# FFN down projection: eight pairs of feature tiles by seven products instead of six, a new order of blocks, the last row of factors in halves

## The chip, the core and the metric

The kernel runs on one core of a Trainium2 chip. Its engines work side by side and are tied together by semaphores: TensorE (PE, with its weight loads shown apart as PEld), VectorE (DVE), ScalarE (ACT), GpSimd (POOL) and SyncE (SP), whose queue issues most transfers. SBUF is the working memory, PSUM holds matmul results (eight banks of 128x512 float32). The metric is the device time of one execution in microseconds (us); lower is better.

## The reference

One transformer layer on 256 latent tokens of width 2048, with 256 context tokens. Everything is float32. The part that matters here is the second half of the layer, the convolutional FFN:

```python
def conv_ffn(h, w_up, conv_w, conv_b, w_down):
    u = depthwise_conv(h @ w_up, conv_w, conv_b)      # width 2 * D_FF, D_FF = 5632
    a, g = jnp.split(u, 2, axis=-1)
    return (jax.nn.silu(g) * a) @ w_down              # (256, 5632) @ (5632, 2048)
...
    h = modulate(rms_norm(x, g_ffn_pre[l]), sh2, sc2)
    x = x + gt2 * rms_norm(conv_ffn(h, w_up[l], conv_w[l], conv_b[l], w_down[l]), g_ffn_post[l])
```

## The kernel before

The layer is one long program; TensorE is fed from its first microseconds to the last. In the order of time: modulation vectors, keys, values, queries, attention, branch products and gates, the output projection, then **FFN up** (from about 775 us to 1264 us) and **FFN down** (from 1264 us to the end).

*Precision.* A float32 matrix is used as a sum of two rounded parts, high and low. `split` (L133) makes them: ACT writes the high part (L137), DVE the low part, source minus high (L141). Each product then takes three matmuls: high by high, low activations by high weights, high activations by low weights (`product`, L1254, matmul at L1256).

*Weights.* They come in blocks of 1 MB (128x2048). `raw_block` (L123) loads one into one of four `raw` buffers; `halves` (L144) splits it into `wh` and `wl`, two buffers each, in two pieces of 128x1024. `block` (L192) hands out the block that is used now and has the next one split and the next three loaded.

*FFN up.* Of the 44 feature tiles of 128 each, `gate` (L1163) makes the gated activations. Tile j lands in `ff` (high and low part, 128 features by 256 tokens), from where it is the stationary operand of the down matmuls. Twelve tiles, J0 = 28 to 39, six pairs, go to `fs` instead, where `gate` stores, for each pair, seven 128x128 combinations of its four quarters (2 tiles by 2 halves of the tokens), four of them made in a small tile `st` by additions (L1183).

*FFN down.* The output, 256x2048, is made in two passes h = 0 and 1, each over two chunks c of 512 columns and two halves t of the tokens: four accumulators C[t, c] in PSUM. A pass takes 22 blocks, whose kinds stand in `SEQ` (L57):

- a **D** block (`direct`, L1260) holds four feature tiles for one chunk: 4 tiles x 2 halves t x 3 = 24 matmuls of 128x512;
- an **S** block (`fold`, L1267) holds one pair of tiles for both chunks. Done directly that would be 2 tiles x 2 chunks x 2 halves = 8 products; by a scheme of Strassen's kind it takes seven, 21 matmuls. Three use `wh`, `wl` as they are (the first 9 matmuls); four use sums of the block's quarters, `th`, `tl`. `folded` (L168) makes those: splits of 128x512 and 128x1024 for `wh`, `wl`, then four additions of 128x512 in place on the raw block (L177), then two splits of 128x1024 into `th`, `tl`, of which there is one buffer each. The seven products go to C[0,0], C[0,1], C[1,0] and four helpers X[1], X[5], X[6], X[7].

```python
SEQ = "DSDDSDDSDDSDDSDDSDDDDD"            # 57
def is_folded(j): return J0 <= j < J0 + 2 * NS   # 64
```

After the last S of a pass (the 17th block, n = 16) `sums_1` and `sums_2` (L1295, L1300) add the helpers up, with ACT and DVE, into the output rows `yg`. `close` (L1283) ends one accumulator: it adds the helper sum, squares with a running sum (ACT, L1291) for the norm, and multiplies by the row `grow` of factors (L1293). In pass 1 C[1,1] gets its helper sum by an addition in PSUM (L1316), before more matmuls go into it. Pass 1 ends with a tail (L1328): the last `lead` = 2 D blocks do t = 0 first, then t = 1, so that half of the output can be finished (`finish`, L1232: norm, residual `x1`, store) under the rest.

PE, DVE and ACT each run their instructions in the order that a scheduler fixed when the program was built; it may move an instruction of one block past those of the next.

Of the kernel before, what the change touches and what calls it, by code (L numbers as in the profile page):

```python
# [10 lines left out]
F32 = mybir.dt.float32  # L11
F32R = mybir.dt.float32r
AF = mybir.ActivationFunctionType
ALU = mybir.AluOpType

P = 128
D = 2048
KT = D // P
S = 256
# [6 lines left out]
FT = DFF // P  # L26
# [26 lines left out]
ND = 4  # L53
SW = (KT - ND) * P // 4
KW = (NKVA + NHB) * P
J0, NS = 28, 6
SEQ = "DSDDSDDSDDSDDSDDSDDDDD"  # L57


def direct_tile(j):  # L60
# [8 lines left out]
def layer_kernel(ctx, tc, xc, xt, ccol, crow, wm_sc, wm_sd, wm_sh, wm_b, cols, wk, wkt, ws, rope, mask_a, bias_b, out):  # L69
    nc = tc.nc  # L70
    sync = nc.sync

    cp = ctx.enter_context(tc.tile_pool(name="cp", bufs=1))
# [9 lines left out]


    col = cp.tile([P, NCOL], F32, name="col")
    cc = cp.tile([P, KT, 32], F32, name="cc")
    ident = cp.tile([P, P], F32, name="ident")
    modx = cp.tile([P, 64], F32, name="modx")
    gcol = cp.tile([P, 2, KT], F32, name="gcol")
# [27 lines left out]
    ggd = tc.dram_tile([2, KT, P], F32, name="ggd")  # L117
# [141 lines left out]
    def gain_row(i, dst):  # L259
        sync.dma_start(out=dst, in_=ggd[i].rearrange("a b -> (a b)").partition_broadcast(P))  # L260
# [10 lines left out]
    with ExitStack() as mx:  # L271
# [10 lines left out]
        with ExitStack() as at:  # L282
# [16 lines left out]
            st = kv.enter_context(ExitStack())  # L299
# [317 lines left out]
            for k in range(3, KT):  # L617
# [2 lines left out]
                        nc.vector.tensor_tensor(out=kT[:, NK1 + i], in0=pk[i][:], in1=rs[:], op=ALU.mult)  # L620
                whole(k)
            st.close()

# [525 lines left out]
        return u, add_halves(u[:], pu, f"u{f}")  # L1151

    def conv(u, f, i):
        a = cv.tile([P, S], F32, tag=f"a{i}", bufs=3 - i, name=f"a{f}")
        cw = [col[:, C_CW + 3 * f + q : C_CW + 3 * f + q + 1] for q in range(3)]
        nc.scalar.activation(a[:], u[:], AF.Identity, scale=cw[1], bias=col[:, C_CB + f : C_CB + f + 1])
        nc.vector.scalar_tensor_tensor(
            out=a[:, 1:], in0=u[:, : S - 1], scalar=cw[0], in1=a[:, 1:], op0=ALU.mult, op1=ALU.add)
        nc.vector.scalar_tensor_tensor(
            out=a[:, : S - 1], in0=u[:, 1:], scalar=cw[2], in1=a[:, : S - 1], op0=ALU.mult, op1=ALU.add)  # L1160
        return a

    def gate(j, a, g):  # L1163
        nc.scalar.activation(g[:], g[:], AF.Silu)
        nc.vector.tensor_tensor(out=a[:], in0=a[:], in1=g[:], op=ALU.mult)
        if not is_folded(j):
            d = direct_tile(j)
            split(ff[:, d, 0], ff[:, d, 1], a[:])
            return
        p, odd = divmod(j - J0, 2)  # L1170
        w = (1 + odd) * P
        hi, lo = (fs[:, p, q].rearrange("p i t -> p (i t)") for q in range(2))
        split(hi[:, odd * P : odd * P + w], lo[:, odd * P : odd * P + w], a[:, :w])
        if not odd:
            first[:] = [a]
            return
        a0, a1 = first[0][:, :P], first[0][:, P:]
        t = cv.tile([P, 4 * P], F32, tag="st", bufs=1, name=f"st{p}")
        t_ = [t[:, i * P : i * P + P] for i in range(4)]
        for o, x, y, op in (  # L1180
            (t_[2], a0, a1, ALU.subtract), (t_[0], a1, a[:, P:], ALU.add), (t_[1], t_[0], a0, ALU.subtract),
            (t_[3], a[:, :P], t_[1], ALU.subtract)):
            nc.vector.tensor_tensor(out=o, in0=x, in1=y, op=op)  # L1183
        split(hi[:, 3 * P :], lo[:, 3 * P :], t[:])
# [55 lines left out]

    first_wts = block(3)
    yg = yp.tile([P, 2, D], F32, name="yg2")
    grow = yp.tile([P, D], F32, name="grow2")
    gain_row(1, grow)
    down = [j for j in range(FT) if not is_folded(j)]
    for h in range(2):
        c0, c1 = 2 * h, 2 * h + 1
# [12 lines left out]
        def direct(wts, g, c, t):  # L1260
            for kk in range(4):
                j = direct_tile(down[4 * g + kk])
                product(
                    C[t, c], lambda i: ff[:, j, i, t * P : t * P + P], *wts, slice(kk * 512, kk * 512 + 512), (t, c),
                    stop=g == 7 and kk == 3)

        def fold(wts, p):  # L1267
            (wh, wl), (th, tl) = wts
# [11 lines left out]
        def add(out_, a, b):  # L1280
            nc.vector.tensor_tensor(out=out_, in0=a, in1=b, op=ALU.add)

        def close(t, c, part, after=None):  # L1283

            y = yg[:, t, cs[c]]
            if part:
                add(y, C[t, c][:], y)
            with ExitStack() as es:
                if after:
                    es.enter_context(tc.issue_after(after))  # L1290
                nc.scalar.activation(  # L1291
                    C[t, c][:] if part else y, y if part else C[t, c][:], AF.Square, accum_out=ss[:, t, c0 + c : c0 + c + 1])
            nc.vector.tensor_tensor(out=y, in0=y if part else C[t, c][:], in1=grow[:, cs[c]], op=ALU.mult)  # L1293

        def sums_1():  # L1295
            nc.scalar.activation(yg[:, 0, cs[0]], X[1][:], AF.Copy)
# [4 lines left out]
            add(yg[:, 0, cs[1]], X[5][:], yg[:, 1, cs[1]])  # L1301
            add(yg[:, 1, cs[1]], X[5][:], yg[:, 1, cs[0]])

        late, d, f, lead = [], 0, 0, 2 * h
        for n, kind in enumerate(SEQ[: len(SEQ) - lead]):
            wts = first_wts if h == n == 0 else block(3)
            if late:
                late.pop(0)()
            if kind == "S":
                fold(wts, f)  # L1310
                f += 1
                if f == NS:
                    late = [sums_1, sums_2, lambda: close(0, 0, True), lambda: close(1, 0, True)]
                    if h:
                        sync.dma_start(out=x1, in_=x1d)
                        late[2:] = [lambda: (close(0, 0, True), add(C[1, 1][:], C[1, 1][:], yg[:, 1, cs[1]]), close(1, 0, True))]  # L1316
            else:
                for t in range(2):
                    direct(wts, d % 8, d // 8, t)
                d += 1  # L1320
            if h and n == 4:
                warm_table(AF.Sqrt, "d", ss[:, 0, 0:1])
        if h == 0:
            for t in range(2):
                close(t, 1, True)
        else:
            wts, after = [], None
            for g in range(8 - lead, 8):  # L1328
                wts.append(block(3))
                direct(wts[-1], g, 1, 0)  # L1330
            for t in range(2):
                if t:
                    for i, g in enumerate(range(8 - lead, 8)):
                        direct(wts[i], g, 1, 1)
                close(t, 1, t == 0, after)
                after = finish(t)


# [30 lines left out]
def _layout(x, c, ctx, c_ctx, w_mod, b_mod, g_attn_pre, g_attn_post, g_ffn_pre, g_ffn_post,  # L1369
# [37 lines left out]
    def slabs(w, n):  # L1407
        k = 2048 // n
        return w.reshape(-1, k, P, w.shape[1] // n, n).transpose(3, 0, 2, 1, 4).reshape(-1, P, 2048)
# [22 lines left out]
    ws[B_UP + 5 : B_DN : 2] = u[FT + 2 :]  # L1432
    wd = f(w_down)[0].reshape(FT, P, D)
    down = [j for j in range(FT) if not is_folded(j)]
    d = slabs(wd[down].reshape(-1, D), 512).reshape(2, 16, P, 2048)
    for h in range(2):
        n, g = iter(range(16)), iter(range(NS))
        for i, kind in enumerate(SEQ):
            if kind == "D":
                ws[B_DN + h * len(SEQ) + i] = d[h, next(n)]  # L1440
            else:
                j = J0 + 2 * next(g)
                a, b = (wd[k][:, h * 1024 : h * 1024 + 1024].reshape(P, 2, 512) for k in (j, j + 1))
                ws[B_DN + h * len(SEQ) + i] = np.concatenate([a[:, 1], a[:, 0], b[:, 1], b[:, 0]], axis=1)
# [26 lines left out]
```

## Time and profile before

| | us |
|---|---|
| three runs: median (lowest to highest) | 1506.01 (1505.78 to 1507.14) |
| the profiled execution: its own time | 1505.69 |
| its span in the trace | 1503.9 |
| FFN down on PE: first to last matmul's start | 1264.2 to 1495.7 |

In the table of the span in 40 slices (each row one engine, a digit the busy share in tenths) PE and its clock stand at 9 throughout; DVE has 9s only within the first eleven slices:

```profile
PE   9999999999999999999999999999999999999997
DVE  4496897999988888877678887887888878777776
PEclk9999999999999999999999999999999999999999
```

A busy PE does not mean that it can go no faster, since matmuls overlap each other; how far apart their starts lie is what counts. Rows of a timeline read: start, length, engine, line, operation, what is written from what, how many in a row, and in brackets how long the engine was idle before and who ended it.

### The profile page before, as it was taken

The numbers are of one execution on the slowest core, as the hardware profiler recorded it, in microseconds if no ns is written. First come the engines' busy times: TensorE is split into PE (matmuls) and PEld (weight loads), VectorE is DVE, ScalarE is ACT, GpSimd is POOL, SyncE is SP. The second block draws the span as 40 slices with busy tenths as digits, with TensorE's granted clock in tenths as the row PEclk, the third lists the DMA queues.
The fourth block names the chain that finished last, engine by engine and source line by source line (L and its number), as shares of the span: only waits on it lengthen the run. The fifth ranks groups of instructions, "written<-read, shape, count | busy, mean of one in ns | idle before, by whom it ended". The sixth has DMA issues, their size and how long they took to land.

```text
span 1503.9 us, 21730 instructions
## 1 busy us (share of the span) xinstructions
PE 1492.0 (99%) x8513; PEld 1282.2 (85%) x8513; DVE 1202.0 (80%) x1797; ACT 800.7 (53%) x1309; POOL 1.6 (0%) x10
## 2 busy tenths in 40 slices
PE   9999999999999999999999999999999999999997
PEld 7876889898888888888888888888888888888886
DVE  4496897999988888877678887887888878777776
ACT  4342532777764554454467555555555565455443
POOL 0000000000000000000000000000000000000000
PEclk9999999999999999999999999999999999999999
DMA  9988779754468888878846666666766655645653
GB/s 366 396 322 335 278 285 343 275 171 167 142 229 299 321 322 324 299 278 323 348 182 217 247 237 237 244 236 221 252 228 234 213 194 179 241 174 194 234 238 112
DMA packets 59254, 381.08 MB, mean 253 GB/s; under 512 B 6544, under 2 KB 6928, under 8 KB 17040
## 3 DMA queue, kind: packets, MB, share of 16 engines
q1 hardware_dynamic: 58432, 378.63, 67.8%
q8 instruction: 67, 1.10, 0.3%
q10 hardware_dynamic: 720, 1.07, 0.2%
q14 instruction: 35, 0.29, 0.1%
HBM read 375.43 MB, written 4.24 MB: 252 GB/s over the span
## 4 chain that ended last, share of the span: by engine, by line
PE 97%; DMA 1%; DVE 1%; ACT 1%; issue 0%; DVEq 0%; ACTq 0%
PE pu L204 21%; PE c L1256 13%; PE pu L205 11%; PE pv L686 7%; PE pg L204 7%; PE pk L468 7%; PE py_o L913 6%; PE pq L204 4%; PE pb L204 4%; PE pg L205 4%; PE pq L205 2%; PE x L1256 2%; PE pb L205 2%; PE po L823 1%; PE s L793 1%; PE pm L342 1%
## 5 line engine op out<-in xcount | busy, mean ns | idle before, releaser
L141 DVE TENSOR_TENSOR wl<-raw,wh 128x1024 fp32r<-128x1024 f32 (+1 forms) x444 | 523.4, 1207 | 141.4 <-ACT wh L137 141.1
L137 ACT ACTIVATE wh<-raw 128x1024 fp32r<-128x1024 f32 (+1 forms) x444 | 446.5, 1041 | 221.8 <-PE c L1256 58.3
L204 PE MATMUL pu<-h,wh 128*128 128x512 f32 x1404 | 488.1, 391 | 0.0
L205 PE MATMUL pu<-h,wl 128*128 128x256 f32 x1404 | 395.9, 282 | 0.0
L204 PEld LDWEIGHTS pu<-h,wh 128*128 128x128 f32 x1404 | 263.6, 188 | 55.6 <-issue 0.4
L205 PEld LDWEIGHTS pu<-h,wl 128*128 128x128 f32 x1404 | 265.4, 189 | 0.0
L204 PE MATMUL pg<-h,wh 128*128 128x512 f32 x464 | 161.5, 390 | 0.0
L1256 PE MATMUL c<-wh,ff 128*128 128x512 f32 x512 | 158.1, 389 | 0.0
L205 PE MATMUL pg<-h,wl 128*128 128x256 f32 x464 | 130.8, 282 | 0.0
L234 DVE SCALAR_TENSOR_TENSOR raw<-raw,crb 128x2048 f32<-128x2048 f32 x48 | 109.7, 2286 | 12.5 <-DMA raw<-in_wm_b_dram 11.9
L468 PE MATMUL pk<-h,ku 128*128 128x512 f32 x480 | 118.1, 398 | 0.9 <-DVE ku L141 0.4
L1256 PEld LDWEIGHTS c<-wh,ff 128*128 128x128 f32 x512 | 96.1, 188 | 19.8
L209 ACT ACTIVATE half_u<-pu 128x256 f32<-128x256 f32 x88 | 33.5, 382 | 147.2 <-PE pu L205 147.2
L468 PEld LDWEIGHTS pk<-h,ku 128*128 128x128 f32 x480 | 87.5, 188 | 25.6 <-issue 4.8
L204 PE MATMUL pq<-h,wh 128*128 128x512 f32 x304 | 108.6, 395 | 0.0
L204 PEld LDWEIGHTS pg<-h,wh 128*128 128x128 f32 x464 | 87.1, 188 | 18.2
L686 PE MATMUL pv<-wh,h 128*128 128x512 f32 (+1 forms) x384 | 101.7, 354 | 0.0
L1256 PE MATMUL c<-wl,ff 128*128 128x512 f32 x256 | 99.8, 390 | 0.0
L204 PE MATMUL pb<-h,wh 128*128 128x512 f32 x256 | 89.4, 390 | 0.0
L205 PEld LDWEIGHTS pg<-h,wl 128*128 128x128 f32 x464 | 87.7, 189 | 0.0
L205 PE MATMUL pq<-h,wl 128*128 128x256 f32 x304 | 85.5, 281 | 0.0
L913 PE MATMUL py_o<-wh,zz 128*128 128x512 f32 x256 | 78.7, 389 | 0.0
(229 smaller groups left out, 2009.2 us busy)
## 6 DMA issues: line engine op xcount, KB each, us to landing
raw<-in_ws_dram SPq DMA_DIRECT2D x222, 1024.0 KB, 4.9
raw<-in_wm_b_dram SPq DMA_DIRECT2D x64, 1024.0 KB, 4.9
raw<-in_wm_sc_dram SPq DMA_DIRECT2D x15, 1024.0 KB, 8.0
raw<-in_wm_sh_dram SPq DMA_DIRECT2D x16, 768.0 KB, 6.3
raw<-in_wkt_dram SPq DMA_DIRECT2D x10, 1024.0 KB, 6.3
raw<-in_wk_dram SPq DMA_DIRECT2D x7, 768.0 KB, 8.5
crb<-sild SPq DMA_DIRECT2D x4, 1024.0 KB, 7.9
sd<-in_wm_sd_dram SPq DMA_DIRECT2D x4, 1024.0 KB, 7.6
```

The source lines that it names most:

```text
L137: a_ = nc.scalar.activation(hi, src, AF.Copy)
L141: v_ = nc.vector.tensor_tensor(out=lo, in0=src, in1=hi, op=ALU.subtract)
L204: nc.tensor.matmul(pt[:, :], wh[:, w], a, start=first and i == 0, stop=False, skip_group_check=True)
L205: nc.tensor.matmul(pt[:, :S], wl[:, w], a[:, 0], start=False, stop=last and i == n - 1, skip_group_check=True)
L209: a_ = nc.scalar.activation(t[:], pt[:, S:], AF.Copy)
L234: nc.vector.scalar_tensor_tensor(out=r, in0=r, scalar=1.0, in1=row, op0=ALU.mult, op1=ALU.mult, accum_out=modx[:, j : j + 1])
L342: nc.tensor.matmul(pm[32 * j : 32 * j + 32, t * P : t * P + P], cc[:, q, :], rsc[k + t][:, q * P : q * P + P], start=q < 4, stop=q >= KT - ...
L468: nc.tensor.matmul(pk[:], wt[:, w], hh[:, :, k, a], start=k == 0 and a == 0 and wt is wh, stop=k == KT - 1 and a == 1)
L686: nc.tensor.matmul(pv[i][:, :nw], src[:, k, a, t0 : t0 + P], wt[:, w], start=k == 0 and q == 0, stop=k == KT - 1 and q == 2)
L793: nc.tensor.matmul(s_ps[:], qs[hd][:, a, qt * P : qt * P + P], k_, start=q == 0, stop=q == 2)
L913: p_ = nc.tensor.matmul(py[t][:], act[:, k, a, t * P : t * P + P], wt[:, w], start=k == 0 and q == 0, stop=k == nk - 1 and q == 2)
L1256: nc.tensor.matmul(pt[:], a(i), wt[:, w], start=k not in begun, stop=stop and q == 2, skip_group_check=True)
```

## The change

It makes five edits:

1. `J0, NS` go from 28, 6 to 24, 8: tiles 24 to 39, eight pairs, are done by seven products. The D blocks of a chunk go from 8 to 7 (`ND0`), so that a pass still has 22 blocks: 14 D and 8 S instead of 16 D and 6 S.
2. `SEQ` becomes another string: in places S, D, S follow each other, with one D between two S where there were two. The last S is n = 17.
3. Room in SBUF: `fs` grows and `ff` shrinks; `st` moves to a PSUM bank (a `bank` buffer); the second conv buffer `a1` goes from two to one; `cc` (the conditioning in columns, used in the first phase) moves from the front of the pool `cp` to a pool of its own at the other end of SBUF that closes after that phase.
4. The row of factors `grow` (2048 wide, loaded once) becomes a row of 1024 in one buffer, loaded for each pass: for pass 1 it is loaded during that pass, after the last use in pass 0.
5. Closing: at the end of pass 0 the helper sums are added to both C[t,1] first, their squares are written to X[5] and X[7], and the two products with `grow` stand in the next pass's second block (`scaled`). In pass 1 `sums_2` and the addition into C[1,1] come together at n = 19, and C[0,0], C[1,0] are closed in the tail.

```diff
-J0, NS = 28, 6
-SEQ = "DSDDSDDSDDSDDSDDSDDDDD"
+J0, NS = 24, 8
+ND0 = (FT - 2 * NS) // 4
+SEQ = "DSDSDSDDSDSDDSDSDSDDDD"
...
-    cc = cp.tile([P, KT, 32], F32, name="cc")
+    ccs = ExitStack()
+    cc = ccs.enter_context(tc.tile_pool(name="ccp", bufs=1, side="right")).tile([P, KT, 32], F32, name="cc")
...
             st.close()
+            ccs.close()
...
-        a = cv.tile([P, S], F32, tag=f"a{i}", bufs=3 - i, name=f"a{f}")
+        a = cv.tile([P, S], F32, tag=f"a{i}", bufs=3 - 2 * i, name=f"a{f}")
...
-        t = cv.tile([P, 4 * P], F32, tag="st", bufs=1, name=f"st{p}")
+        t = bank(f"st{p}")
...
-    grow = yp.tile([P, D], F32, name="grow2")
-    gain_row(1, grow)
+    late, rows = [], {}
+
+    def row_of(h):
+        rows[h] = yp.tile([P, 1024], F32, tag="grow2", bufs=1, name=f"grow2_{h}")
+        sync.dma_start(out=rows[h], in_=ggd[1, 8 * h : 8 * h + 8].rearrange("a b -> (a b)").partition_broadcast(P))
+
+    row_of(0)
...
-        def close(t, c, part, after=None):
+        def close(t, c, part, after=None, junk=None):
             y = yg[:, t, cs[c]]
-            if part:
+            if part == 1:
                 add(y, C[t, c][:], y)
...
-                    C[t, c][:] if part else y, y if part else C[t, c][:], AF.Square, accum_out=ss[:, t, c0 + c : c0 + c + 1])
-            nc.vector.tensor_tensor(out=y, in0=y if part else C[t, c][:], in1=grow[:, cs[c]], op=ALU.mult)
+                    (junk or C[t, c])[:] if part else y, y if part else C[t, c][:], AF.Square,
+                    accum_out=ss[:, t, c0 + c : c0 + c + 1])
+            if part < 2:
+                nc.vector.tensor_tensor(
+                    out=y, in0=y if part else C[t, c][:], in1=rows[h][:, c * 512 : c * 512 + 512], op=ALU.mult)
...
                 if f == NS:
-                    late = [sums_1, sums_2, lambda: close(0, 0, True), lambda: close(1, 0, True)]
+                    late = [sums_1, sums_2, lambda: close(0, 0, 1), lambda: close(1, 0, 1)]
                     if h:
+                        row_of(h)
                         sync.dma_start(out=x1, in_=x1d)
-                        late[2:] = [lambda: (close(0, 0, True), add(C[1, 1][:], C[1, 1][:], yg[:, 1, cs[1]]), close(1, 0, True))]
+                        late[1:] = [lambda: (sums_2(), add(C[1, 1][:], C[1, 1][:], yg[:, 1, cs[1]]))]
             else:
                 for t in range(2):
-                    direct(wts, d % 8, d // 8, t)
+                    direct(wts, d % ND0, d // ND0, t)
...
         if h == 0:
             for t in range(2):
-                close(t, 1, True)
+                add(yg[:, t, cs[1]], C[t, 1][:], yg[:, t, cs[1]])
+            for t in range(2):
+                close(t, 1, 2, junk=X[5 + 2 * t])
...
+            late = [lambda: None, scaled]
         else:
             wts, after = [], None
-            for g in range(8 - lead, 8):
+            for g in range(ND0 - lead, ND0):
                 wts.append(block(3))
                 direct(wts[-1], g, 1, 0)
+                close(g - ND0 + lead, 0, 1)
```

**DVE between two S blocks of pass 0.** `wl` of 512 opens an S block's preparation, `tl` ends it; the rows with 1024 x2 alone are D blocks. The kernel before, from an S block's preparation (n = 7) to the next S (n = 10):

```order
L141 TENSOR_TENSOR wl_12029<-raw_11973,wh_12028 128x512
L141 TENSOR_TENSOR wl_12029<-raw_11973,wh_12028 128x1024
L177 TENSOR_TENSOR raw_11973<-raw_11973 128x512 x4
L141 TENSOR_TENSOR tl_12031<-raw_11973,th_12030 128x1024 x2
L141 TENSOR_TENSOR wl_12071<-raw_12002,wh_12070 128x1024 x2
L141 TENSOR_TENSOR wl_12100<-raw_12044,wh_12099 128x1024 x2
L141 TENSOR_TENSOR wl_12132<-raw_12076,wh_12131 128x512
```

The same place in the change, from n = 8 (S) to n = 10 (S):

```order
L143 TENSOR_TENSOR wl_12086<-raw_12030,wh_12085 128x512
L143 TENSOR_TENSOR wl_12086<-raw_12030,wh_12085 128x1024
L179 TENSOR_TENSOR raw_12030<-raw_12030 128x512 x4
L143 TENSOR_TENSOR tl_12088<-raw_12030,th_12087 128x1024 x2
L143 TENSOR_TENSOR wl_12128<-raw_12059,wh_12127 128x1024 x2
L143 TENSOR_TENSOR wl_12157<-raw_12101,wh_12156 128x512
```

Between two S preparations there is now one D preparation, not two.

**ACT at the start of FFN down.** `raw_11694` and `raw_11712` are the first S block (n = 1) before and in the change. Before:

```order
L137 ACTIVATE wh_11864<-raw_11748 128x1024
L137 ACTIVATE wh_11893<-raw_11827 128x1024
L137 ACTIVATE th_11813<-raw_11694 128x1024 x2
L137 ACTIVATE wh_11893<-raw_11827 128x1024
L137 ACTIVATE wh_11925<-raw_11870 128x512
```

In the change:

```order
L139 ACTIVATE wh_11882<-raw_11766 128x1024
L139 ACTIVATE wh_11911<-raw_11845 128x512
L139 ACTIVATE wh_11911<-raw_11845 128x1024
L139 ACTIVATE th_11831<-raw_11712 128x1024 x2
L139 ACTIVATE th_11913<-raw_11845 128x1024 x2
```

Block n = 3 was a D, of which one piece came ahead of the first `th`; it is an S, both of whose pieces come ahead of it, and its own `th` follows at once.

**DVE after the last S block of pass 1**, where C[1,1] gets its helper sum. Before (`c_1_12592` is C[1,1], `wl_13218` the block n = 19):

```order
L1281 TENSOR_TENSOR yg_11829<-c_1_12586,yg_11829 128x512
L1293 TENSOR_TENSOR yg_11829<-yg_11829,grow_11830 128x512
L141 TENSOR_TENSOR wl_13218<-raw_13158,wh_13217 128x1024 x2
L1293 TENSOR_TENSOR yg_11829<-yg_11829,grow_11830 128x512
L952 TENSOR_REDUCE r_11809<-ss_11808 128x1 x2
L953 TENSOR_SCALAR r_11809<-r_11809 128x1 x2
L1281 TENSOR_TENSOR c_1_12592<-c_1_12592,yg_11829 128x512
```

In the change (`c_1_12622` is C[1,1], `wl_13298` the first block of the tail):

```order
L1289 TENSOR_TENSOR yg_11847<-c_1_12616,yg_11847 128x512
L1303 TENSOR_TENSOR yg_11847<-yg_11847,grow_1_13259 128x512
L1289 TENSOR_TENSOR c_1_12622<-c_1_12622,yg_11847 128x512
L143 TENSOR_TENSOR wl_13298<-raw_13236,wh_13297 128x1024 x2
L1303 TENSOR_TENSOR yg_11847<-yg_11847,grow_1_13259 128x512
```

The addition into C[1,1] moved ahead of a block's `wl`, of a product and of the small operations of the norm.

More of the change, by code (lines that the diff above doesn't have):

```diff
@@ L1264, in direct @@
                     C[t, c], lambda i: ff[:, j, i, t * P : t * P + P], *wts, slice(kk * 512, kk * 512 + 512), (t, c),
-                    stop=g == 7 and kk == 3)
+                    stop=g == ND0 - 1 and kk == 3)
         def fold(wts, p):
@@ L1302, in sums_2 @@
             add(yg[:, 1, cs[1]], X[5][:], yg[:, 1, cs[0]])
-        late, d, f, lead = [], 0, 0, 2 * h
+        d, f, lead = 0, 0, 2 * h
         for n, kind in enumerate(SEQ[: len(SEQ) - lead]):
@@ L1324, in layer_kernel, with scaled @@
             for t in range(2):
-                close(t, 1, True)
+                add(yg[:, t, cs[1]], C[t, 1][:], yg[:, t, cs[1]])
+            for t in range(2):
+                close(t, 1, 2, junk=X[5 + 2 * t])
+            def scaled(cs=cs):
+                for t in range(2):
+                    nc.vector.tensor_tensor(out=yg[:, t, cs[1]], in0=yg[:, t, cs[1]], in1=rows[0][:, 512:], op=ALU.mult)
+            late = [lambda: None, scaled]
         else:
             wts, after = [], None
-            for g in range(8 - lead, 8):
+            for g in range(ND0 - lead, ND0):
                 wts.append(block(3))
                 direct(wts[-1], g, 1, 0)
+                close(g - ND0 + lead, 0, 1)
             for t in range(2):
                 if t:
-                    for i, g in enumerate(range(8 - lead, 8)):
+                    for i, g in enumerate(range(ND0 - lead, ND0)):
                         direct(wts[i], g, 1, 1)
-                close(t, 1, t == 0, after)
+                close(t, 1, 1 - t, after)
                 after = finish(t)
@@ L1434, in _layout @@
     down = [j for j in range(FT) if not is_folded(j)]
-    d = slabs(wd[down].reshape(-1, D), 512).reshape(2, 16, P, 2048)
+    d = slabs(wd[down].reshape(-1, D), 512).reshape(2, 2 * ND0, P, 2048)
     for h in range(2):
-        n, g = iter(range(16)), iter(range(NS))
+        n, g = iter(range(2 * ND0)), iter(range(NS))
         for i, kind in enumerate(SEQ):
```

## The prediction

> **What bounds the kernel now.** I read the page's busy times and the chain that ended last first.
>
> ```profile
> span 1503.9 us, 21730 instructions
> PE 1492.0 (99%) x8513; PEld 1282.2 (85%) x8513; DVE 1202.0 (80%) x1797; ACT 800.7 (53%) x1309; POOL 1.6 (0%) x10
> ```
>
> ```profile
> PE 97%; DMA 1%; DVE 1%; ACT 1%; issue 0%; DVEq 0%; ACTq 0%
> ```
>
> 97% of the chain is TensorE's. What the change moves lies in FFN down, so that stretch decides, by three questions: how far apart matmuls start, whether PE waits there for anyone, and how late the engine that feeds it is. The view of line L1256 (all down matmuls) answers the second, the timeline of PE the first.
>
> ```profile
>   DVE wl L141: 0.6, 2
>   DVE tl L141: 0.4, 2
> ```
>
> ```profile
> 1285.73 0.62 PE L1256 MATMUL x<-wh,fs 128*128 128x512 f32 x2
> ...
> 1290.49 0.62 PE L1256 MATMUL c<-wh,ff 128*128 128x512 f32 x2
> ...
> 1301.37 0.62 PE L1256 MATMUL x<-wh,fs 128*128 128x512 f32 x2
> ```
>
> The first two rows are the idle time ahead of down matmuls by who ended it: 1.0 us in all, of PE's weight loads. The others are the first matmuls of an S block, of the first of two D blocks, and of the next S: 4.76 and 10.88 us apart. For 21 and 48 matmuls that is **0.2267 us a matmul** both times, so PE is the bound.
>
> **What goes.** FFN down has 16 x 2 x 24 + 6 x 2 x 21 = 1020 matmuls; 14 x 2 x 24 + 8 x 2 x 21 = 1008 remain. Twelve are gone: 12 x 0.2267 = **2.72 us**, all on the path. The view of the line gives lengths, and the first and last start:
>
> ```profile
> L1256 PE MATMUL c<-wh,ff x512: 388/389/397, 1264.2 to 1495.5; 128*128 128x512 f32 x171
> ...
> L1256 PE MATMUL c<-wl,ff x256: 388/389/499, 1264.7 to 1495.7; 128*128 128x512 f32 x128
> ```
>
> Twelve times 0.389 is 4.67, but neighbours overlap, and only the distance of starts is time: 1019 distances of 0.2267 make 231.0 us, and from 1264.2 to 1495.7 it was 231.5. The Trainium skill, "TensorE: Matmul & The Clock Gate", Back-to-back issue gap, gives N/2.4 + 2.5 ns for an isolated gap, 216 ns at 512 columns; by it the gain would be an estimated 2.59 us, and the trace is near it. The same section has 131 ns as the sustained figure of a stream of load and matmul; by that the gain would be an estimated 1.57 us. The trace contradicts it with 227 ns.
>
> **What the extra S blocks add, on DVE.** The preparation of an S block that follows two D blocks, and of the two D blocks behind it (the S block starts at 1301.37):
>
> ```profile
> 1296.57 0.69 DVE L141 TENSOR_TENSOR wl<-raw,wh 128x512 fp32r<-128x512 f32 x1 [2.97 <-ACT wh L137]
> 1297.52 1.23 DVE L141 TENSOR_TENSOR wl<-raw,wh 128x1024 fp32r<-128x1024 f32 x1 [0.26 <-ACT wh L137]
> 1298.78 2.87 DVE L177 TENSOR_TENSOR raw<-raw 128x512 f32<-128x512 f32 x4
> 1302.05 2.36 DVE L141 TENSOR_TENSOR tl<-raw,th 128x1024 fp32r<-128x1024 f32 x2 [0.40 <-ACT th L137]
> 1304.33 4.63 DVE L141 TENSOR_TENSOR wl<-raw,wh 128x1024 fp32r<-128x1024 f32 x4
> ```
>
> ```profile
> 1295.90 1.58 ACT L137 ACTIVATE wh<-raw 128x512 fp32r<-128x512 f32 x2 [4.50 <-PE c L1256]
> ```
>
> An S block costs DVE 7.84 us (1296.57 to 1304.41), two `wl` of a D block 2.27 (half of four pitches, (4.63 - 1.22) / 3 = 1.14 each). Before, S, D, D took PE 15.64 us, and DVE idled 2.97 of them. Where the change has S, D, S, PE takes 10.20 and DVE 10.11 by these rows. That looks too close, but the 0.26 and the start at 1296.57 come from ACT, which waited for a buffer that the D block before last held (the ACT row). In S, D, S the same buffer was held by the previous S, which lets it go after its first 9 matmuls, so ACT is ahead. Then DVE runs through: 2.27, then 0.61 (0.69 less the overlap) + 1.14 + 2.93 (2.87 and the gaps beside it) + 0.43 (ACT's first `th`) + 2.27, together 9.7 us from one `tl` to the next. I take **9.7** (the place below shows no gap but that one); the bounds are 9.7 and 10.2, the latter with every wait and no overlap left (full durations 0.69 + 1.23 + 2.87 + 2.36 + 2.36, waits 0.66).
>
> How late may `tl` be? The only place where PE waited in mid-course, the first S block of pass 1:
>
> ```profile
> 1385.69 0.61 PE L1256 MATMUL x<-wh,fs 128*128 128x512 f32 x2
> ...
> 1387.73 0.61 PE L1256 MATMUL x<-th,fs 128*128 128x512 f32 x2
> 1388.18 0.49 PE L1256 MATMUL x<-tl,fs 128*128 128x512 f32 x1
> ```
>
> ```profile
> 1383.63 2.86 DVE L177 TENSOR_TENSOR raw<-raw 128x512 f32<-128x512 f32 x4
> 1386.90 2.36 DVE L141 TENSOR_TENSOR tl<-raw,th 128x1024 fp32r<-128x1024 f32 x2 [0.40 <-ACT th L137]
> 1389.17 2.35 DVE L141 TENSOR_TENSOR wl<-raw,wh 128x1024 fp32r<-128x1024 f32 x2
> ```
>
> Here the second `tl` ended 3.57 us after the block's first matmul, and the matmul on `tl` took 0.49 instead of 0.39: a stall of 0.10. (The first `tl` ended at 1388.12, PE wanted it at 1388.18 and went on 0.10 later, so DVE's end reaches PE after 0.16.) So up to 3.47 us costs nothing. Behind two D blocks it is 3.04 (1304.41 - 1301.37), a slack of 0.43. From there each S, D pair wins 10.20 - 9.7 = 0.5, so the next S stands at 2.5, the one after at 2.0: **no stall**. At the bound of 10.2 nothing is won and nothing lost. In the first S of pass 1 the order of DVE and ACT is as before; its stall of 0.10 stays.
>
> **The start of FFN down.** There ACT and DVE are still behind with the last gates, and the change lets the S block n = 3 go ahead of the first `th`.
>
> ```profile
> 1272.51 2.35 DVE L141 TENSOR_TENSOR wl<-raw,wh 128x1024 fp32r<-128x1024 f32 x2
> ```
>
> ```profile
> 1271.73 0.61 PE L1256 MATMUL c<-wh,ff 128*128 128x512 f32 x2
> ...
> 1274.34 1.52 PE L1256 MATMUL x<-th,fs 128*128 128x512 f32 x6
> ```
>
> Before, one piece of 1024 stood between block 2 and `th`/`tl`; now 512 and 1024 do. ACT: `th` starts 0.55 later, 1273.4 and ends at 1275.4; DVE: 512 from 1273.65, 1024 from 1274.26, `tl` from 1275.40, ready at 1276.62 and 1277.76. PE also has two more matmuls of block 2 ahead of `th`, so it comes there at 1274.80, to the second piece of `th` at 1275.70, and by the order of its rows to `tl` at 1276.84 and 1277.97. With the 0.16 that leaves 0.06 and 0.05 us. Block 3 then: additions from 1277.8, `tl` done at 1282.35 and 1283.48, wanted at 1282.73 and 1284.09. Nothing is lost by my value; if each of these is 0.3 late, 0.6 us. The stalls ahead of it, on block 2's `wl`, are untouched: ten matmuls from 1271.73 to 1274.34, 0.34 over their pitch.
>
> **The end.** The addition into C[1,1] must now be done before the second half of block 19, not of a later point in DVE's order.
>
> ```profile
> 1468.76 0.62 PE L1256 MATMUL c<-wh,ff 128*128 128x512 f32 x2
> ...
> 1471.50 2.08 DVE L1281 TENSOR_TENSOR yg<-x,yg 128x512 f32<-128x512 f32 x3
> ...
> 1475.49 0.68 DVE L1293 TENSOR_TENSOR yg<-yg,grow 128x512 f32<-128x512 f32 x1
> ...
> 1479.84 0.70 DVE L1281 TENSOR_TENSOR c<-c,yg 128x512 f32<-128x512 f32 x1 [0.48 <-PE c L1256]
> ```
>
> The first row is the first D after the last S. DVE's helper sums began 2.74 us behind it, the product followed at 6.73 to 7.33; the addition comes next, to 8.0. One D block sooner after the last S than before, PE wants it at 5.44 + 2.72 = 8.16. With the 0.16 that is even; in the change the sums start some 0.4 sooner, since `tl` of the last S stands at 2.0 and not 3.0. Value 0; bounds 0 and 1.0 (DVE a `wl` later). Behind the addition on DVE wait the `wl` of the tail's blocks, which have 2 us.
>
> **What is hidden.** `st` in PSUM, one `a1` buffer and two more folded pairs fall into FFN up:
>
> ```profile
> 1050.00:1262.00 212.00, 212.00 (x1225) 187.94 (x1224) 171.27 (x274) 123.36 (x200) 0.00 (x0) 1.00 0.61 219
> ```
>
> ```profile
> L1183 DVE TENSOR_TENSOR st<-a,st 128x128 f32<-128x128 f32 x6 | 1.7, 285 | 0.0
> ```
>
> PE is busy all of the 212 us of the first row (a late stretch of FFN up, the six folded pairs among it), DVE 171. A folded pair adds four additions as in the last row and a wider split, some 1.5 us, to two tiles that take PE 22 (88 steps in the 488 us of FFN up); DVE idles 4.2 in those. `a1` is read by its gate a step (5.5 us) before the next one is written, so one buffer is enough. If this cover went, each folded pair would cost up to 1.5. The half row for pass 1 stands in SP's queue behind the fifth block's load and waits for two products early in pass 1; the next load waits longer, for the first S block's `raw`. X[5] and X[7] take squares that DVE's products ahead of 1383.63 have waited for; X[5] is first written at 1387.73. `cc`'s move shifts tiles by 2 KB; all distances in the front stay. I cost all this at 0. The tail behind the last matmul keeps its operations.
>
> **The sum.** The profiled execution took 1505.69, 1.8 over its span and 0.32 under the median. 1505.69 - 2.72 = 1502.97; at the median **1503.3**, which is 0.18% less.
>
> **Rivals.**
> - *More goes than the matmuls.* If the changed order also takes the stalls at the start and in pass 1 (0.34 + 0.10), the time is 1502.9; with a median as low in its scatter as 1505.78 is, 1502.6. For: PE reaches the first `th` 0.45 later. Against: the `wl` that cost most is made in the same order. 0.14.
> - *Part is given back.* `tl` late by 0.3 at the start's two places (0.6) and C[1,1] by 0.5: 1504.4. For: the slacks of 0.05 and 0 above. Against: the sooner start of the sums. 0.14. By the 131 ns that the Trainium skill gives in the section above the time would be an estimated 1504.4 too; the trace bears that out nowhere, so it gets no chance of its own.
> - *DVE becomes the bound and the kernel slower.* The place is the ten S, D, S steps, in six runs, two of which (first in each pass) have no slack, four 0.43. For a chain of x us a step the loss is 10 (x - 10.2) - 1.7. To eat the gain x must be 10.64; to be slower by 0.2%, 10.94, that is DVE 13% slower than its rows; at 15% (11.15) the loss is 7.8 and the time 1511.1. For: every tile lies elsewhere. Against: `wl` of 1024 takes 1.21 to 1.23 in every stretch of the trace. 0.06.
> - That the change doesn't save the matmuls can't be: PE's rows hold twelve fewer.
>
> **How the numbers follow.** Forecast 0.66, the rivals 0.14, 0.14, 0.06. About 0.2% (3.0 us) is what a measurement here can tell from no change; the bound is 1503.0, only 0.3 under the forecast, and the three runs before scatter by 1.4. A quarter of the forecast's chance falls below it: faster 0.17 + 0.12 = 0.29, same 0.65, slower 0.06. The range goes from 1502.0 (first rival, with its scatter) to 1505.2: the bounds of the start and of C[1,1] together, 1.6, and 0.3 of scatter.
>
> **What would show it.** 1008 matmuls in FFN down at 0.227, the last starting near 1493; S, D, S steps 10.2 apart without idle time for `tl`; the addition into C[1,1] ahead of PE. I am wrong if PE's idle time for DVE in the down lines is over 2 us, or if `wl` of 1024 takes over 1.3.

## The result, and the profile after

Over 20 executions each, the changed kernel took **1503.20 us** (median; 1502.84 to 1506.01), the kernel before 1505.86 (1505.42 to 1507.85): 2.66 us less, a ratio of 0.9985 with a 95% interval of 0.9978 to 0.9991. The forecast was 1503.3.

The page of the changed kernel, span and busy times:

```profile
span 1502.6 us, 21696 instructions
PE 1489.4 (99%) x8501; PEld 1279.6 (85%) x8501; DVE 1221.0 (81%) x1831; ACT 806.8 (54%) x1319; POOL 1.6 (0%) x10
```

Twelve matmuls fewer (8501 for 8513), TensorE's busy time 2.6 us less, VectorE's 19 us more. The view of the line of the down matmuls (L1264 now), with the idle time ahead of them by who ended it:

```profile
L1264 PE MATMUL c<-wh,ff x448: 388/389/397, 1265.3 to 1493.9; 128*128 128x512 f32 x150
...
L1264 PE MATMUL c<-wl,ff x224: 388/389/499, 1265.8 to 1494.1; 128*128 128x512 f32 x112
...
  DVE wl L143: 0.6, 2
  DVE tl L143: 0.3, 1
```

FFN down now lasts from 1265.3 to 1494.1, 228.8 us from the first to the last start where it was 231.5: **2.7 us less**, twelve distances of 0.2267. The idle time is that of the kernel before, `wl` at the start and `tl` in the first S block of pass 1, and no third place has come.

Yet this profiled execution took 1504.36, only 1.33 less than the one before. It lost 1.1 us long before FFN down, in attention. The timelines of ACT and PE there, of the changed kernel, and then ACT's row at the same place in the kernel before:

```profile
273.19 1.06 ACT L139 ACTIVATE wh<-raw 128x1024 fp32r<-128x1024 f32 x1 [1.79 <-DMA raw<-in_ws_dram]
```

```profile
282.90 0.96 PE L796 MATMUL s<-h 128*128 128x512 f32 x3 [1.13 <-DVE h L143]
```

```profile
271.77 2.01 ACT L137 ACTIVATE wh<-raw 128x1024 fp32r<-128x1024 f32 x2 [1.16 <-DMA raw<-in_ws_dram]
```

A weight block landed 1.4 us later than in the profile before, and 10 us on TensorE waited 1.13 us for what VectorE made behind it. This wait differs from execution to execution: the second profile of the kernel before (below) has 0.36 us of it; of the twelve profiles of kernels with the new layout six have none and six have 0.3 to 1.1; and one kernel, that of six pairs below, has none in its first profile and 0.84 in its second. So the profiles are compared stage by stage, and the whole times by their medians.

### The profile page after: what moved, and what is told of

Its sections match the earlier page's. It is cut to its first block, busy times and chain, and to the rows that moved or that the text cites. A ratio compares the mean times of both kernels' runs of the same rounds, so it can differ in the third digit from the quotient of the medians.

```text
span 1502.6 us, 21696 instructions
## 1 busy us (share of the span) xinstructions
PE 1489.4 (99%) x8501; PEld 1279.6 (85%) x8501; DVE 1221.0 (81%) x1831; ACT 806.8 (54%) x1319; POOL 1.6 (0%) x10
## 4 chain that ended last, share of the span: by engine, by line
PE 91%; DVE 4%; DMA 3%; issue 1%; ACT 1%; DVEq 0%; SPq 0%; ACTq 0%
PE pu L206 21%; PE c L1264 12%; PE pu L207 11%; PE pk L470 7%; PE pg L206 7%; PE py_o L916 6%; PE pb L206 4%; PE pg L207 4%; PE pq L206 4%; PE x L1264 3%; PE pb L207 2%; PE pq L207 2%; DMA raw<-in_wm_b_dram 2%; PE pv L689 1%; PE po L826 1%; PE s L796 1%
## 5 line engine op out<-in xcount | busy, mean ns | idle before, releaser
L1264 PE MATMUL c<-wh,ff 128*128 128x512 f32 x448 | 137.8, 389 | 0.0
L1264 PEld LDWEIGHTS c<-wh,ff 128*128 128x128 f32 x448 | 84.0, 188 | 17.3
L1264 PE MATMUL c<-wl,ff 128*128 128x512 f32 x224 | 87.4, 390 | 0.0
```

The source lines that it names most:

```text
L1264: nc.tensor.matmul(pt[:], a(i), wt[:, w], start=k not in begun, stop=stop and q == 2, skip_group_check=True)
```

## The experiments

All of them, with the two kernels. "FFN down" is from the first to the last matmul's start; "store" is the time from the issue of the last store to its landing, by the view of the DMA queues; both of one profile each. The kernel before was run again beside each group of experiments, with medians of 1505.7 to 1506.0; a ratio is to those executions, not to the first row.

| kernel | median (lowest to highest), runs | ratio to before (95%) | FFN down | store |
|---|---|---|---|---|
| before | 1505.86 (1505.42 to 1507.85), 20 | | 231.5 | 2.5 |
| changed | 1503.20 (1502.84 to 1506.01), 20 | 0.9985 (0.9978 to 0.9991) | 228.8 | 2.7 |
| before once more | 1506.12 (1505.15 to 1508.20), 11 | 1.0002 (0.9993 to 1.0010) | 231.5 | 2.4 |
| six pairs, other edits kept | 1507.05 (1506.44 to 1509.09), 11 | 1.0006 (0.9997 to 1.0015) | 231.6 | 2.9 |
| the same again | 1507.29 (1506.64 to 1508.34), 11 | 1.0010 (1.0001 to 1.0018) | 231.6 | 3.5 |
| four pairs | 1509.46 (1508.61 to 1511.03), 9 | 1.0023 (1.0014 to 1.0033) | 234.3 | 2.7 |
| S at n = 1, 3, ..., 15 | 1503.89 (1503.26 to 1506.00), 11 | 0.9986 (0.9977 to 0.9995) | 228.8 | 3.0 |
| S at n = 2, 4, ..., 16 | 1503.21 (1502.75 to 1505.17), 11 | 0.9981 (0.9973 to 0.9990) | 228.3 | 3.0 |
| `wl` of 512 twice | 1504.45 (1504.05 to 1507.72), 11 | 0.9994 (0.9985 to 1.0003) | 230.0 | 2.7 |
| `wl` of 1024 twice | 1508.44 (1508.05 to 1509.79), 11 | 1.0019 (1.0011 to 1.0028) | 233.6 | 2.7 |
| S blocks in pairs | 1514.79 (1514.18 to 1516.02), 5 | 1.0052 (1.0039 to 1.0065) | 239.4 | 3.4 |
| a helper sum five times | 1504.92 (1504.52 to 1509.46), 12 | 0.9991 (0.9983 to 1.0000) | 229.8 | 2.6 |
| n = 2, ..., 16, SP shifted | **1502.09** (1501.81 to 1502.94), 5 | 0.9968 (0.9956 to 0.9980) | 228.3 | 2.1 |
| six pairs, SP shifted | 1506.02 (1505.44 to 1507.32), 11 | 0.9995 (0.9987 to 1.0004) | 231.6 | 2.1 |

### Is it the count of matmuls?

Six pairs in the new layout, and four:

```diff
-J0, NS = 24, 8
-SEQ = "DSDSDSDDSDSDDSDSDSDDDD"
+J0, NS = 28, 6
+SEQ = "DSDDSDDSDDSDDSDDSDDDDD"
```

> The changed kernel with six pairs again (tiles 28 to 39, 16 D and 6 S blocks a pass in the old order of blocks), all its other edits kept: the half rows of factors, `st` in PSUM, one `a1` buffer, `cc` in its own pool, the new closing. Theory (the whole difference is twelve matmuls at 0.2267 us each, the other edits are worth nothing): FFN down on TensorE has 1020 matmuls again and takes 231.5 us from first to last start as in the kernel before (228.8 with eight pairs); 1505.9 us, within 0.3 of the kernel before. Rival (layout or closing have a share of the 2.7 us): the time stands between, 0.5 us or more under 1505.9.

```diff
-J0, NS = 24, 8
-SEQ = "DSDSDSDDSDSDDSDSDSDDDD"
+J0, NS = 32, 4
+SEQ = "DSDDDSDDDSDDDSDDDDDDDD"
```

> The changed kernel with four pairs (tiles 32 to 39; 18 D and 4 S blocks a pass, an S block after every three D blocks). Theory (time goes with the count of matmuls): 18 x 2 x 24 + 4 x 2 x 21 = 1032 matmuls, 24 more than with eight pairs, 24 x 0.2267 = 5.4 us: 1508.6 us, FFN down 234.2 us from first to last start. Rival (the S blocks' preparation or the folded gates in FFN up already cost something, so that fewer of them give some of it back): under 1508.0 us.

The down matmuls of six pairs, then of four:

```profile
L1264 PE MATMUL c<-wh,ff x512: 388/390/398, 1264.0 to 1495.4; 128*128 128x512 f32 x171
...
L1264 PE MATMUL c<-wl,ff x256: 387/390/501, 1264.5 to 1495.6; 128*128 128x512 f32 x128
```

```profile
L1264 PE MATMUL c<-wh,ff x576: 388/390/398, 1264.9 to 1499.0; 128*128 128x512 f32 x192
...
L1264 PE MATMUL c<-wl,ff x288: 387/390/502, 1265.4 to 1499.2; 128*128 128x512 f32 x144
```

FFN down took 231.6 us with 1020 matmuls and 234.3 with 1032, beside 228.8 with 1008: 2.8 and 2.7 for twelve each. In this stage the theory holds, and the other edits are worth 0.1. The whole time did not follow: six pairs stood 1.1 us above the kernel before and 3.9 above the changed one, four pairs 0.9 above the forecast. Neither theory had it. Six pairs are taken up below, under the last store. For four pairs it stays open: their last store lands as in the changed kernel (2.7), but in their profile FFN down began at 1264.9, 0.7 later than in the first profile of the kernel before, and 0.31 of that is the wait in attention. Their lowest time of nine, 1508.61, is the forecast.

### Does the order of the blocks matter?

```diff
-SEQ = "DSDSDSDDSDSDDSDSDSDDDD"
+SEQ = "DSDSDSDSDSDSDSDSDDDDDD"
```

> The changed kernel with eight S blocks a pass at n = 1, 3, 5, 7, 9, 11, 13, 15, so that seven S, D, S steps follow each other with no two D blocks among them; the count of matmuls is unchanged. Theory (VectorE needs 9.76 us for such a step and TensorE 10.20, so VectorE gains 0.44 a step): no idle time of TensorE for `tl` beyond the two places of the changed kernel; the same time within 0.3, 1503.2 us. Rival (VectorE lives on the reserve that two D blocks in a row give, a step costs over 10.2): a loss of 0.2 us or more in each of the last steps of a run of seven, 1505 us or more.

FFN down is the same to 0.1 us, with idle time in the same two places: no loss in runs of seven steps. The median is 0.7 higher, of which 0.3 is the later landing of the last store (3.0 for 2.7); the rest is not told apart from scatter.

```diff
-SEQ = "DSDSDSDDSDSDDSDSDSDDDD"
+SEQ = "DDSDSDSDSDSDSDSDSDDDDD"
```

> The changed kernel with the S blocks at n = 2, 4, 6, 8, 10, 12, 14, 16: each pass begins with two D blocks. Theory (what is left of idle time in FFN down, 0.35 us at 1273 to 1275 and 0.10 in the first S block of pass 1, comes from the first S block's additions, which stand on VectorE between the last gates and the next block's `wl`): both places go, FFN down takes 228.4 us from first to last start instead of 228.8, 1502.8 us. Rival (the gates of the last tiles keep VectorE late whatever block comes first): the idle time stays at 0.3 us or more and the time at 1503.2 us.

The view of the line, whose list of waits is now empty, and VectorE at the first S block:

```profile
L1264 PE MATMUL c<-wh,ff x448: 389/389/395, 1264.4 to 1492.4; 128*128 128x512 f32 x150
...
L1264 PE MATMUL c<-wl,ff x224: 388/389/393, 1264.8 to 1492.6; 128*128 128x512 f32 x112
...
its engine sat idle before it (us, times) until:
who waited for it (us, times):
```

```profile
1271.06 0.42 DVE L143 TENSOR_TENSOR ff<-a,ff 128x256 fp32r<-128x256 f32 x1
1271.71 1.23 DVE L143 TENSOR_TENSOR wl<-raw,wh 128x1024 fp32r<-128x1024 f32 x1 [0.23 <-ACT wh L139]
1272.97 2.87 DVE L179 TENSOR_TENSOR raw<-raw 128x512 f32<-128x512 f32 x4
```

The additions now come behind the last gate's `ff` and the `wl`, and both places of idle time are gone: 228.3 us. The median did not move: 0.3 of the 0.5 us was lost again because the last store landed later (3.0 for 2.7), and the other 0.2 is within the scatter.

```diff
-SEQ = "DSDSDSDDSDSDDSDSDSDDDD"
+SEQ = "DSSDDSSDDSSDDSSDDDDDDD"
```

> The changed kernel with the S blocks in pairs (n = 1, 2, 5, 6, 9, 10, 13, 14: S, S, D, D), the same count of matmuls. Theory (VectorE's chain decides where S follows S: it needs 9.76 - 2.27 = 7.5 us from one `tl` to the next and TensorE 4.76, with a reserve of 0.43 behind two D blocks): 2.3 us of idle time in each of eight pairs, 18.4 in all, 1521.6 us, within 3. Rival (VectorE's 81% of the span say that it has room, the order of blocks is of no matter): 1503.2 us.

```profile
  DVE wl L143: 9.3, 14
  ACT th L139: 5.0, 10
  DVE tl L143: 3.9, 10
```

The same number of matmuls cost 11.6 us more, 10.6 of it in FFN down. So the order decides, though less than expected, and most of the idle time stands ahead of `wl`, not `tl` (the rows count the waits of the weight loads with those of the matmuls). The scheduler had sorted the program for this order: TensorE's rows run the first nine matmuls of the second S block right behind those of the first, and fill in D matmuls between the products on `th` and `tl`. The 18.4 us had been worked out with the order held still.

### How near is VectorE to being the bound?

```diff
             split(h[:, q], lo[:, q], r[:, q])
+        nc.vector.tensor_tensor(out=lo[:, sl[1]], in0=r[:, sl[1]], in1=h[:, sl[1]], op=ALU.subtract)
```

> The changed kernel, in which every S block's preparation computes the 512 columns of `wl` twice on VectorE (0.61 us more for each S block, the same values). An S, D, S step then takes VectorE 9.76 + 0.61 = 10.37 us and TensorE 10.20. Theory A (the prediction's formula, loss = 10 (x - 10.2) - 1.7, the reserve of 0.43 behind two D blocks and the like stay whole): no loss, 1503.2 us. Theory B (the second `tl` may end 3.47 us after its block's first matmul, so the first may start up to 1.11; the extra work stands ahead of every S block, those behind two D blocks too): those start `tl` at 0.68 + 0.61 = 1.29 and lose 0.18, four of them; ten steps lose 0.17 each; the first S block of pass 1 loses 0.6; together 3.0 us, and up to 1.2 more at the start of FFN down: 1506.2 to 1507.4 us.

The other kernel has `1024:` in place of `sl[1]`.

> The changed kernel, in which every S block's preparation computes the 1024 columns of `wl` twice on VectorE (1.14 us more for each S block, the same values): x = 9.76 + 1.14 = 10.90 us a step. Theory A (the prediction's formula): 10 x 0.70 - 1.7 = 5.3 us lost, 1508.5 us. Theory B (the extra work uses up the reserve behind two D blocks as well): four times 0.71, ten times 0.70, 1.1 in the first S block of pass 1, together 11.0 us, and up to 2.3 at the start of FFN down: 1514.2 to 1516.5 us.

VectorE from one S block's `tl` to the next across S, D, S: the changed kernel, then 512 twice, then 1024 twice:

```profile
1307.92 2.36 DVE L143 TENSOR_TENSOR tl<-raw,th 128x1024 fp32r<-128x1024 f32 x2 [0.40 <-ACT th L139]
...
1317.68 1.23 DVE L143 TENSOR_TENSOR tl<-raw,th 128x1024 fp32r<-128x1024 f32 x1 [0.48 <-ACT th L139]
```

```profile
1307.91 2.36 DVE L143 TENSOR_TENSOR tl<-raw,th 128x1024 fp32r<-128x1024 f32 x2 [0.40 <-ACT th L139]
...
1318.14 1.22 DVE L143 TENSOR_TENSOR tl<-raw,th 128x1024 fp32r<-128x1024 f32 x1 [0.48 <-ACT th L139]
```

```profile
1310.46 2.35 DVE L143 TENSOR_TENSOR tl<-raw,th 128x1024 fp32r<-128x1024 f32 x2
...
1316.98 2.87 DVE L180 TENSOR_TENSOR raw<-raw 128x512 f32<-128x512 f32 x4
1319.77 1.22 DVE L143 TENSOR_TENSOR wl<-raw,wh 128x1024 fp32r<-128x1024 f32 x1
1320.90 2.35 DVE L143 TENSOR_TENSOR tl<-raw,th 128x1024 fp32r<-128x1024 f32 x2
```

A step takes 9.76 us in the changed kernel (1307.92 to 1317.68), 10.23 with 0.61 more work and 10.44 with 1.14 more. Part of the extra work costs nothing: with 1024 twice, the scheduler put a `wl` of the next block where VectorE had waited 0.48 us for `th`.

With 512 twice (x = 10.23, 0.03 over TensorE's 10.20) the steps behind the start and behind the first S block of pass 1, those with two D blocks too, lose 0.05 us at most each, as theory A had it. The second `tl` ends 3.2 to 3.45 us behind its block's first matmul there, just inside the 3.47 that the prediction allows. But FFN down grew by 1.2 us: 0.75 at its start, where the waits of the down matmuls for `wl` grew from 0.6 to 1.6 us by the view of their line, 0.25 in the first S block of pass 1, and 0.2 over all those steps. The first two are places that theory B named (up to 1.2, and 0.6). So the whole, 1.25 us, is neither A's nothing nor B's 3.0 to 4.2.

With 1024 twice the time, 1508.44, is what theory A said, 1508.5, but not for its reason: with the measured x of 10.44 its formula gives 10 x 0.24 - 1.7 = 0.7 us, and FFN down grew by 4.8. The waits of the matmuls in that kernel:

```profile
  ACT th L139: 5.9, 26
  DVE wl L143: 2.9, 7
  DVE tl L143: 1.7, 5
```

Of the 4.8 us 0.9 is lost at the start; the rest is spread over the S blocks of all kinds: S, D, S steps took TensorE 10.4 to 10.6 us, and S, D, D, S ones 15.8 to 15.9 instead of 15.64. So the reserve behind two D blocks was used up by the same work, as theory B says: every step lost 0.2 to 0.4. B's mechanism is right and its size wrong, because the chain did not grow by what was put into it.

### The place of the addition into C[1,1]

```diff
-            add(yg[:, 0, cs[1]], X[5][:], yg[:, 1, cs[1]])
+            for _ in range(1 + 4 * h):
+                add(yg[:, 0, cs[1]], X[5][:], yg[:, 1, cs[1]])
```

> The changed kernel with one of the helper sums of pass 1 computed five times (four more additions of 128x512 with the same values); by VectorE's order a block's two `wl` then also stand ahead of the addition into C[1,1], as in the prediction's bound for that place. Theory (TensorE waits for that addition at the second half of block 19, 8.16 us behind the last S block's end; it ended at 7.13 in the changed kernel, a reserve of 0.87 with 0.16 for the way; now it ends at about 11.1): 3.1 us of idle time there, 1506.3 us. Rival (the scheduler puts other matmuls ahead, or the tail takes it up): under 1 us lost, 1504.2 us or less.

VectorE and TensorE at that place in the changed kernel, then with the sum five times:

```profile
1474.47 2.08 DVE L1289 TENSOR_TENSOR yg<-x,yg 128x512 f32<-128x512 f32 x3
...
1479.06 0.69 DVE L1289 TENSOR_TENSOR c<-c,yg 128x512 f32<-128x512 f32 x1
```

```profile
1472.62 0.61 PE L1264 MATMUL c<-wh,ff 128*128 128x512 f32 x2
```

```profile
1484.98 0.70 DVE L1289 TENSOR_TENSOR c<-c,yg 128x512 f32<-128x512 f32 x1
```

```profile
1485.74 0.72 PE L1264 MATMUL c<-wh,ff 128*128 128x512 f32 x2 [0.39 <-DVE c L1289]
```

TensorE does wait for that addition: the row starts 0.06 us behind its end and lasts 0.11 longer than such a pair does (0.72 for 0.61), so TensorE goes on 0.17 behind it, near the 0.16 of the prediction. But the loss was 1.7 us, not 3.1 (0.95 in FFN down, of which some two thirds here and the rest at two waits for the tail's blocks; 0.55 behind the last matmul): the scheduler had put one more half block ahead of it on TensorE, so that the wait stands 10.9 us behind the last S block, not 8.16. Both theories were half right.

### The last store, and what six pairs lost

The tails gave the hint. (TensorE's last digit in the table of the span is 7, not 9 as the text ahead of the prediction has it: 8.2 us behind the last matmul's start still belong to the span.) The operations behind the last matmul are the same in all kernels, but the last store's landing is not. First the kernel before and the six pairs were run again.

> The kernel before once more, unchanged, for a second profile of it. From the last matmul's start to the end of the span it took 8.2 us in its first profile, and 8.4 to 8.9 us in the five profiles of kernels with the new layout; the six pairs in the new layout measured 1507.05 us where 1505.9 was expected. Theory (the last store's landing differs from execution to execution, and the profile of six pairs shows FFN up's end and FFN down where they were, so that its extra 1.1 us is scatter): this profile's tail lies anywhere from 8.1 to 8.9 us, its FFN down at 231.5 us, its time within 0.3 of 1505.97 us. Rival (the new layout's stores land later): 8.2 us again, within 0.1.

> Six pairs in the new layout, the same kernel again beside the kernel before. Theory (the 1.1 us by which it stood above the kernel before is scatter of executions, mostly ahead of FFN down): 1506.0 us, within 0.5 of the kernel before; FFN down 231.6 us. Rival (the other edits cost about 1.1 us with six pairs): 1507 us again, its lowest time again 1 us above the lowest of the kernel before.

The rivals held: the kernel before had its early landing again (2.4), and six pairs were 1.5 us slower again. The view of the DMA queues, from 4.7 to 6.4 us behind the last matmul's start; first the kernel before (1500.4 to 1502.1), then six pairs in the second profile (1501.6 to 1503.3). A row is a queue (packets, MB, share of the time of 16 DMA engines) or an issue (KB, us to landing):

```profile
q10 hardware_dynamic: 144, 0.26, 42.1%
issues: line engine op xcount, KB each, median us to landing
out_dram<-yg SPq DMA_DIRECT2D x1, 256.0 KB, 2.5
```

```profile
q14 instruction: 1, 0.01, 4.5%
issues: line engine op xcount, KB each, median us to landing
out_dram<-yg SPq DMA_DIRECT2D x1, 256.0 KB, 3.5
```

A transfer of kind "instruction", 8 KB on queue 14, stands among the last stores of all kernels with the new layout, and not in this stretch of the kernel before, where it comes as the last packet ends. Of such transfers there are 36 in the changed kernel (section 3 of its page). To see whose code it is, fifteen instructions were added to SyncE's stream alone:

```diff
-        sync.dma_start(out=rows[h], in_=ggd[1, 8 * h : 8 * h + 8].rearrange("a b -> (a b)").partition_broadcast(P))
+        for i in range(1 if h else 16):
+            w = slice(None) if h else slice(64 * i, 64 * i + 64)
+            sync.dma_start(
+                out=rows[h][:, w],
+                in_=ggd[1, 8 * h : 8 * h + 8].rearrange("a b -> (a b)")[w].partition_broadcast(P))
```

> The kernel with the S blocks at n = 2, 4, ..., 16 (1503.21 us, no idle time left in FFN down), in which the half row of factors for pass 0 is loaded by sixteen small transfers instead of one: 15 more instructions in SP's stream, nothing else. In all profiles with the new layout a code load of 8 KB (queue of kind instruction) starts 5.1 to 5.5 us behind the last matmul's start, among the last stores, whose last packet ends 6.95 to 7.84 us behind it; in the two profiles of the kernel before it starts at 6.57, when the last packet has just ended (6.57). Theory (the load is SP's own: it comes at SP's row 721 to 723 of some 731, so 15 instructions more put it some 20 us ahead of the stores): no code load among the last stores, the last packet ends at 6.6, the tail is 8.2 us instead of 8.75 and the time 1502.7 us. Rival (the landing of the last stores has another cause, such as the new place of the output rows): the tail stays at 8.4 us or more and the time at 1503.2 us.

> Six pairs in the new layout (1507.05 and 1507.29 us, 1.1 and 1.5 above the kernel before, with FFN down only 0.1 longer), with the same sixteen small transfers instead of one. Theory (the code load among the last stores is what it lost: their last packet ended 7.2 and 7.8 us behind the last matmul's start instead of 6.57): it ends at 6.6, the tail is 8.2 us, the time 1506.0 to 1506.5 us. Rival (the other edits cost 1.1 us elsewhere): 1507.1 us as before.

```profile
q10 hardware_dynamic: 144, 0.26, 42.0%
issues: line engine op xcount, KB each, median us to landing
out_dram<-yg SPq DMA_DIRECT2D x1, 256.0 KB, 2.1
```

No such transfer is left in the tail of either (the rows are those of the order n = 2, ..., 16), the last store lands after 2.1 us, and the medians fall by 1.0 to 1.3 us, to 1502.09 and 1506.02. The load itself is still there: it comes when SyncE is at the same place of its rows (the 720th to 722nd, for the 721st without the fifteen), but that place is now reached 47 and 51 us ahead of the last matmul's start, and the other loads of code in the last 100 us kept theirs to 1.4 us (all by the packets of the traces). So it is SyncE's code. By the landing, the load cost the changed kernel 0.6 us and six pairs 0.8 to 1.4. The kernel before stands 0.3 to 0.4 above the 2.1 as well, with its load as the last packet ends; that this is the load's doing is likely but not shown, as it was not run with SyncE's code shifted.

What is left of six pairs' loss is the 0.1 in FFN down and some 0.35 us outside the span: the time of an execution is 2.1 to 2.2 us above its span in all 33 executions of six pairs, and 1.7 to 1.9 in those of all other kernels. With the 0.5 and 1.1 us by which the two profiles end later behind the last matmul, that makes 0.9 and 1.55 of the 1.1 and 1.5 us. Why the time outside the span grew stays open.

## Why the prediction was right, and where it was not

- **Twelve matmuls at 0.2267 us.** Right: FFN down lost 2.7 us, and the two steps to six and to four pairs cost 2.8 and 2.7. Of the two figures of the Trainium skill, "TensorE: Matmul & The Clock Gate", Back-to-back issue gap, the isolated one (216 ns) is near the trace, the sustained one (131 ns) is not.
- **VectorE in the dense places.** "I take 9.7": 9.76 by the trace. Behind the start TensorE waited for VectorE in no S, D, S step but the first of pass 1 (0.1 us), not even in runs of seven, and in the changed kernel `tl` stood 0.44 earlier after each.
- **The start.** PE was to come to `th` at 1274.80 and `tl` to begin at 1275.40. With the 1.1 us by which this execution was late, that is 1275.90 and 1276.50; TensorE's first product on `th` began at 1275.92, VectorE's `tl` at 1276.49. The waits for block 2's `wl` stayed, as forecast.
- **The addition into C[1,1].** Taken as even, with a gain of 0.4 from the sooner sums. They began 1.85 us behind the last S block, not 2.74, so 0.9 sooner, as the second `tl` of that block ended 2.2 us behind its first matmul, not 3.0. The gain was sized at half of what it is, and the addition ended at 1479.75, 7.13 behind the block's end at 1472.62: 1.03 short of the 8.16, a reserve of 0.87 after the 0.16 of the way to TensorE.
- **What was hidden.** FFN down began 1.1 us later than before, and TensorE's wait in attention was 1.13. From TensorE's first row on `pu`, just ahead of FFN up, to FFN down's first matmul it was 498.8 us in both profiles: two more folded pairs cost FFN up nothing.
- **The tail, the failed step.** "The tail behind the last matmul keeps its operations" holds for the operations, but one more instruction or two in SyncE's queue moved a load of its code in among the last stores. It cost the change 0.2 us (2.7 for 2.5), small enough to go unseen in the sum; with six pairs the same thing cost up to 1.0. By the stages of the two profiles the change is worth 2.7 less 0.2, so 2.5 us; the medians differ by 2.66. That the forecast of 1503.3 came within 0.1 is in part luck.
- **More goes than the matmuls**: didn't come, because the first S block's additions kept their place. The order with S at n = 2, ..., 16 shows that 0.5 us was there to be had.
- **VectorE as the bound**: the formula's condition was wrong. It kept the reserve of 0.43 for the growing chain, where whatever lengthens the preparation uses that up too. With x at 10.44, below the 10.64 from which the gain was to be gone, the kernel was slower than before.

The best kernel here has eight pairs, S at n = 2, ..., 16 and SyncE's code shifted: 1502.09 us, 0.9968 (0.9956 to 0.9980) of the kernel before, from five executions. Ten pairs were not tried.

## What to carry to other kernels

On a saturated TensorE a removed matmul is worth the distance of starts, not its length, and the gain is sure only as far as the engine that prepares the operands keeps its time per step: find the step with the least room, and the wait at which its reserve ends. A cost that is worked out with the order held still can come out too high where a scheduler sorts the program anew (18.4 us where FFN down lost 10.6, 3.1 where it lost 0.95), and its waits turn up in other places than expected. Before the edits of a change are charged with a microsecond of unclear origin, compare the tails: a store that lands later may only share the queue with a load of code.

## What the runs showed of the hardware

An engine's code comes in by DMA while it runs, and that can be late work on the critical path: with 8 KB among the last stores a store of 256 KB landed after 2.6 to 3.5 us, without them after 2.1 (and after 2.4 to 2.5 in the kernel before, where they come as the last packet ends). The Trainium skill, "Runtime: NRT & Kernel Launch", Instruction fetch mechanics, has the sequencer load its next page by DMA while the present one runs, in blocks of 16 KiB, at a cost "mostly hidden". The traces agree on the way, and have 8 KB blocks on queue 14 beside 16 KB ones on queue 8 (section 3 of the page: 36 with 0.29 MB, 67 with 1.10 MB):

```profile
q8 instruction: 67, 1.10, 0.3%
...
q14 instruction: 36, 0.29, 0.1%
```

In FFN down of the order n = 2, ..., 16 twelve such loads ran, and TensorE lost nothing to them: 1007 distances of 0.2267 make 228.3 us, which it took. The one among the last stores did cost, since no work was left for the late store to hide behind. For the rest of the program no run shows what a load of code costs.
